# Moving a layer's modulation loads ahead of its linear attention and loading ready-made bias tables, in a two-layer diffusion trunk

## The chip, the cores and the metric

The kernel runs on one core of one Trainium2 chip. The metric is the device time of one execution in microseconds. Before the change three runs took 1935.68, 1934.28 and 1926.67 us, a median of 1934.28 us.

## The reference

Two layers are applied to 512 latent tokens and 256 context tokens of width 1024, in float32. Each layer mixes tokens by four groups of heads, writes them out by one projection, and ends in a feed-forward block with a convolution in its gate. Cut to what matters here:

```python
for l in range(DEPTH):                       # DEPTH = 2
    ctx_out = l < DEPTH - 1
    mod_l = silu(c) @ w_mod[l] + b_mod[l]    # six vectors of 1024: shift, scale, gate of mixing and of ffn
    mod_c = silu(c_ctx) @ w_mod[l] + b_mod[l]
    hl = rmsnorm(xl, g_pre_mix[l]) * (1 + sc_ml) + sh_ml
    hc = rmsnorm(xc, g_pre_mix[l]) * (1 + sc_mc) + sh_mc
    y_c, y_l = token_mixing(hc @ w_in[l], hl @ w_in[l], ...)     # S5, NA, GLA, SWA side by side
    xl = xl + gt_ml * rmsnorm(y_l @ w_out[l], g_post_mix[l])
    hl = rmsnorm(xl, g_pre_ffn[l]) * (1 + sc_fl) + sh_fl
    xl = xl + gt_fl * rmsnorm(conv_ffn(hl, ...), g_post_ffn[l])
    ...

def na_mixer(...):       # neighbourhood attention: an 8 x 64 grid, blocks of 16 columns, 32 key columns each
    bias = rpb[:, dr, dc]                    # by the difference of rows and of columns
    s_nb = einsum("brnqhd,brnkwhd->bhrnqkw", ql, k_blk) * scale + bias
    s_nb = where(in_win, s_nb, -1e30)        # 16 columns around the query
    s_cx = einsum("brnqhd,bchd->bhrnqc", ql, kc) * scale
    p_nb, p_cx = joint_softmax(s_nb, s_cx)
```

The first third of the modulation (shift and scale ahead of mixing) is wanted at once; the other two thirds, rounds 1 and 2 in the kernel, hold the gate of mixing and what the feed-forward block needs, and are wanted only after `w_out`.

## The kernel before

`mixing` runs a layer's token mixing in stages, one behind the other: the linear attention (GLA, with `gla_core`), the state-space model (S5, eight units made by `s5_unit`), neighbourhood attention (NA, `na_units`, two pairs of heads, four column blocks and the context for each), and windowed attention (SWA). In layer 0 GLA lies at about 164 to 264 us, S5 at 264 to 330 and NA at 330 to 427. The products of the input projection that later stages need are no stage of their own: `project` (L789) queues them as generators in `self.fill`, and `gap(n)` draws n of their steps between the pieces of the attention code, so that PE has work while VectorE (DVE) and ScalarE (ACT) run a softmax or a scan. `need(name)` draws a projection to its end. A second list, `self.later`, holds the modulation: each `gap` ends with `pump(self.rate)`, which takes `rate` steps from it. The rates are r00 in GLA, r01 in S5 and r02 in NA for layer 0 (2, 1 and 2).

`mod_round` (L206) makes one round of modulation: 32 steps, each with one 256 KB load into `wm` (L215, on SP's queue, three buffers) and four matmuls (L218) into one PSUM bank; `mod_end` copies the sum (`modrow`, L226) and transposes it (`modt`, L229). Rounds 1 and 2 of layer 0 become available at `mods()` (L1405 and L1445 in `mixing`), which before stands at the beginning of S5, so that their 64 steps are drawn in S5 and NA; a `pump(1000)` at the beginning of SWA draws what is left. PSUM has eight banks in three groups: two for the dense sums (tag "d"), four for the attentions' inner products (tag "m"), and two for their outputs (tag "o"). The modulation's sum takes one with tag "o".

`run_units` (L539) runs a list of units in a pipeline: it starts a unit, calls `gap`, and then carries the unit before to its next piece. In S5 a unit's first half makes `bu` (L853), its second half `s5o` (L884), copies that to `s5zz` (L885, two buffers of its own) and stores it. `s5_end` loads the stored result, loads `w_glu` (L901, ACT's queue), and applies the gate.

`na_table` (L974) makes the bias of one head: eight loads of 24 KB from a padded copy of `na_rpb` (`nawide`, L981, ACT's queue), each with a window that slides by partition, and three adds on GpSimd (POOL, L985) of a window mask that is loaded once a layer (`namask`, L1477). `na_units` makes two tables for each pair of heads, copies the queries from row order into block order (`nqb`, L1057, ACT), and then yields four units (`na_unit`: scores `nas` L1028, table add and maximum L1034, exponential L1036, transposition `napt` L1043, output `nao` L1049). The rotary tables of SWA's `rope` are loaded on ACT's queue (L1075).

The order of instructions on each engine is not written out by hand: a scheduler sets it, by a simulated timeline, from the order of the program, the waits and the buffers. Names in the rows: `pd` is a dense sum, `gA` and `go` GLA's scores and outputs, `gS` its state, `gms` its norm, `lap` and `la` its gates, `tp` a transposition, `gp` SWA's gate rows, `co` and `cs` the context attention, `glu` S5's gate, `pka` S5's operands, built by the kernel and kept in `s5ops` in device memory.

Of the kernel before, what the change touches and what calls it, by code (L numbers as in the profile page):

```python
# [10 lines left out]
FT = mybir.dt.float32  # L11
# [25 lines left out]
KN = dict(build=(1, 1, 1, 2, 1, 1, 1, 1, 2, 1, 1), build1=0, r00=2, r01=1, r02=2, r10=0, r11=3, r12=1, glaA=1, glaB=1, s5=2, s5b=2, na1=0, na2=1, sw1=1, sw2=2, swA=4, pump=6, rows=2, d4=2, ahead=3000, s5n=3, gt=2, six=1, bg=1, wat=(0, 2, 4, 6), wmb=5, go0=12, s5e=4, resA=1, resB=0, slow=1, slow0=5, ro1=2, ro2=2)  # L37
# [4 lines left out]
C_SP, C_SN, C_NA, C_COS, C_SIN, C_ALL = 384, 512, 640, 1408, 1920, 2432  # L42
# [17 lines left out]
def constants():  # L60
    c = np.zeros((128, C_ALL), np.float32)
    i = np.arange(128)
    c[:, C_ID:C_ID + 128] = np.eye(128)
    same = (i[:, None] // 64) == (i[None, :] // 64)
    c[:, C_BD:C_BD + 128] = same / 64.0
    c[:, C_G:C_G + 64] = i[:, None] % 64 <= i[None, :64]
    c[:, C_G + 64:C_G + 128] = i[:, None] % 64 >= i[None, :64]
    c[:, C_SP:C_SP + 128] = np.where(i[None, :] >= i[:, None], 0.0, NEG)
    c[:, C_SN:C_SN + 128] = np.where(i[None, :] <= i[:, None], 0.0, NEG)
    for t, b in enumerate((0, 1, 3)):  # L70
        col = 16 * b + i % 16
        ws = np.clip(col - 8, 0, 48)
        kc = NA_OFF[b] + np.arange(256) % 32
        ok = (kc[None, :] >= ws[:, None]) & (kc[None, :] < ws[:, None] + 16)
        c[:, C_NA + 256 * t:C_NA + 256 * (t + 1)] = np.where(ok, 0.0, NEG)
    t = np.arange(512)
    inv = (np.float32(10000.0) ** (-np.arange(0, 32, 2, dtype=np.float32) / np.float32(32))).astype(np.float32)
    d = i % 64
    pos = np.where((d < 32)[:, None], (t // 64)[None, :], (t % 64)[None, :]).astype(np.float32)
    ang = (pos * inv[d % 16][:, None]).astype(np.float32).astype(np.float64)  # L80
    c[:, C_COS:C_COS + 512] = np.cos(ang)
    c[:, C_SIN:C_SIN + 512] = np.sin(ang) * np.where((d % 32) < 16, -1.0, 1.0)[:, None]
    return c


class Trunk:
# [118 lines left out]
    def mod_round(self, l, r, pool, tag="o"):  # L205
# [6 lines left out]
        for i in range(4 * KT):  # L212
            k, c = i // 4, i % 4
            w = pool.tile([128, 512], FT, name="wm", tag="wm", bufs=3)
            nc.sync.dma_start(w, self.a["w_mod"][l, 128 * k:128 * (k + 1), 2048 * r + 512 * c:2048 * r + 512 * c + 512])  # L215
# [323 lines left out]
    def run_units(self, units, gaps):  # L539

        last = None
        for u in list(units) + [None]:
            if u is not None:
                next(u)
            for n in gaps:
# [243 lines left out]
    def project(self, l, H, name, cols, chunks, scale=1.0, o=None):  # L789

        def steps():
            w = self.w_in(l, cols)
            t = self.R[name] = o or self.p3(name)
            for c0, cn in chunks:
                p = self.ps("pd", "d")[:, :cn]
                yield from self.dense_steps(w, H, c0, cn, p)
                self.nc.scalar.mul(t[:, c0:c0 + cn], p, scale)
# [43 lines left out]
    def s5_unit(self, l, r, U, ops, zd, ctx_out):  # L841
# [43 lines left out]
        z = mp.tile([128, 2, 96], FT, name="s5zz", tag="s5zz", bufs=2)  # L885
# [6 lines left out]
    def s5_end(self, l, zd, Y, ctx_out):  # L892
# [8 lines left out]
        nc.scalar.dma_start(wg, a["s5_w_glu"][l].rearrange("(k p) m -> p k m", p=128))  # L901
# [168 lines left out]
    def rope(self):  # L1070
# [3 lines left out]
        for c, o in zip(cs, (C_COS, C_SIN)):  # L1074
            nc.scalar.dma_start(c, self.a["cpack"][:, o:o + 512])  # L1075
# [262 lines left out]
    def mixing(self, l, H, ctx_out):  # L1338
# [66 lines left out]
        mods = lambda: self.later.extend([self.chain([self.mod_round(0, r, self.wm) for r in (1, 2)])] if l == 0 else [])  # L1405
# [46 lines left out]
        mods()  # L1452
# [12 lines left out]
        self.run_units(units, (KN['s5b'] if l else KN['s5'],))  # L1465
# [10 lines left out]
        mk = self.mp.tile([128, NT], FT, name="namask")  # L1476
        nc.scalar.dma_start(mk, a["cpack"][:, C_NA:C_NA + 768])  # L1477
# [375 lines left out]
```

## Time and profile before

| | us |
|---|---|
| median of three runs | 1934.28 |
| the profiled execution | 1929.45 |
| its span in the profile | 1927.7 |
| TensorE (PE) busy, 11705 matmuls | 1790.8 |
| its weight loads (PEld, beside PE) | 1465.3 |
| VectorE (DVE) | 1167.0 |
| ScalarE (ACT) | 727.1 |
| GpSimd (POOL) | 157.3 |

The span is one execution on one core, taken by the hardware profiler. A busy time is the sum of an engine's instructions and says nothing of what waits for what: engines work beside each other. A long busy PE can still be PE at half its speed, so the granted clock is read beside it: 1.00 is 2.4 GHz, 0.50 is 1.2 GHz, and a stretch between has both. The mean over the execution is 0.954. Idle time of an engine counts only where the chain of waits runs through it. Instructions that issue a transfer occupy the issuing engine's queue for a while (SP, ACT and POOL issue here) and the transfer lands later.

### The profile page before, as it was taken

The page shows a single profiled execution, that of the slowest core. Times are in us where ns is not written, and L with a number is a line of the kernel's source. Part 1 is how long each engine was busy: PE and PEld are TensorE (multiplying, and loading weights), DVE is VectorE, ACT ScalarE, POOL GpSimd, SP SyncE. Part 2 cuts the span into 40 slices and gives each one's busy share as a digit, 9 for nine tenths or more (in the row PEclk, how much of TensorE's full clock was granted, in tenths as well). Part 3 has the DMA queues.
Part 4 walks back from the last instruction along what each step waited for, and adds up shares of the span by engine and source line. Part 5 has one row for each costly group of instructions (what it writes and reads, how often), then busy time and mean ns, then how long its engine had stood idle before and what let it go on. Part 6 is the DMA issues. An engine that isn't in the chain of part 4 may idle for free.

```text
span 1927.7 us, 30566 instructions
## 1 busy us (share of the span) xinstructions
PE 1790.8 (93%) x11705; PEld 1465.3 (76%) x11705; DVE 1167.0 (61%) x2793; ACT 727.1 (38%) x1486; POOL 157.3 (8%) x236
## 2 busy tenths in 40 slices
PE   4899989798998999999999997999798989999997
PEld 2888768565678888888888877877576688888885
DVE  5796655653779946864843474766464654444446
ACT  5334412543664323222222254642354643323222
POOL 5121000100111000000000020000100100000001
PEclk7999889898998999999999998999898999999999
DMA  9264146444123434543533132326322043323232
GB/s 305 65 173 128 40 132 188 113 138 133 64 88 116 151 103 137 170 134 112 165 117 99 56 119 91 95 82 174 79 70 78 23 133 112 106 83 114 77 117 79
DMA packets 243185, 219.79 MB, mean 114 GB/s; under 512 B 45324, under 2 KB 187590, under 8 KB 243040
## 3 DMA queue, kind: packets, MB, share of 16 engines
q1 hardware_dynamic: 225600, 198.52, 34.0%
q0 software_dynamic: 6528, 15.06, 2.7%
q10 hardware_dynamic: 10912, 4.26, 1.4%
q8 instruction: 92, 1.51, 0.3%
q14 instruction: 53, 0.43, 0.1%
HBM read 190.27 MB, written 27.53 MB: 113 GB/s over the span
## 4 chain that ended last, share of the span: by engine, by line
PE 78%; DVE 8%; DMA 7%; ACT 3%; issue 2%; SPq 1%; POOL 1%; ACTq 0%; DVEq 0%; POOLq 0%
PE pd L471 28%; PE pd L312 20%; PE pd L482 12%; DMA wm<-in_w_mod_dram 3%; PE pd L509 2%; PE nao L1049 1%; DVE wlo L275 1%; PE swo L1164 1%; PE go L1279 1%; DMA nawide<-in_rpb_pad_dram 1%; DMA pka<-s5ops 1%; PE s5o L884 1%; PE go L1282 1%; PE swpt L1152 1%; PE napt L1043 1%
## 5 line engine op out<-in xcount | busy, mean ns | idle before, releaser
L275 DVE TENSOR_TENSOR wlo<-wst,whi 128x1024 fp32r<-128x1024 f32 x190 | 232.9, 1226 | 247.5 <-ACT whi L274 236.6
L274 ACT CAST whi<-wst 128x1024 fp32r<-128x1024 f32 x190 | 199.5, 1050 | 423.6 <-PE pd L471 124.9
L312 PE MATMUL pd<-whi,hidh 128*128 128x512 f32 x440 | 171.8, 392 | 1.7 <-DVE za L352 1.6
L312 PE MATMUL pd<-whi,hidl 128*128 128x512 f32 x440 | 171.5, 390 | 0.0
L312 PE MATMUL pd<-wlo,hidh 128*128 128x512 f32 x440 | 170.6, 390 | 0.0
L312 PEld LDWEIGHTS pd<-whi,hidh 128*128 128x128 f32 x440 | 82.6, 188 | 20.6 <-DVE za L352 2.9
L312 PEld LDWEIGHTS pd<-wlo,hidh 128*128 128x128 f32 x440 | 82.6, 188 | 17.5
L312 PEld LDWEIGHTS pd<-whi,hidl 128*128 128x128 f32 x440 | 82.6, 188 | 17.1
L196 DVE SCALAR_TENSOR_TENSOR macc<-wm,cT,macc 128x512 f32<-128x512 f32 x112 | 82.3, 748 | 19.6 <-DMA wm<-in_w_mod_dram 18.9
L1578 DVE TENSOR_TENSOR fg<-fg,pd 128x512 f32<-128x512 f32 x64 | 38.5, 602 | 64.8 <-PE pd L471 63.6
L1577 ACT ACTIVATE fg<-fg 128x512 f32<-128x512 f32 x66 | 36.8, 559 | 105.7 <-DVE fg L1576 101.9
L1628 DVE TENSOR_TENSOR za<-za,pd 128x512 f32<-128x512 f32 (+1 forms) x40 | 21.9, 552 | 72.1 <-PE pd L312 72.1
L1574 ACT ACTIVATE fg<-pd,vb 128x512 f32<-128x512 f32 x64 | 39.4, 618 | 46.0 <-PE pd L471 46.0
L363 POOL TENSOR_TENSOR za<-za,g 128x768 f32<-128x768 f32 x10 | 18.8, 1882 | 413.1 <-ACT sq L353 382.9
L1575 DVE SCALAR_TENSOR_TENSOR fg<-pd,vb,fg 128x511 f32<-128x511 f32 x64 | 42.2, 661 | 15.6 <-ACT fg L1574 15.6
L274 ACT CAST hidh<-fg 128x512 fp32r<-128x512 f32 x66 | 36.1, 547 | 36.5 <-DVE fg L1578 36.1
L471 PE MATMUL pd<-h0h,whi 128*128 128x512 f32 (+1 forms) x118 | 43.7, 370 | 4.7 <-DVE fg L1576 2.9
L471 PE MATMUL pd<-h0h,wlo 128*128 128x512 f32 (+1 forms) x118 | 42.4, 359 | 4.5 <-DVE wlo L275 4.5
L275 DVE TENSOR_TENSOR hidl<-fg,hidh 128x512 fp32r<-128x512 f32 x66 | 39.2, 597 | 7.0 <-ACT hidh L274 6.9
L1576 DVE SCALAR_TENSOR_TENSOR fg<-pd,vb,fg 128x511 f32<-128x511 f32 x64 | 42.5, 663 | 1.2
L218 PE MATMUL modp<-wm,cT 128*32 128x128 f32 x512 | 28.9, 313 | 14.9 <-DMA wm<-in_w_mod_dram 12.8
L471 PE MATMUL pd<-h1h,whi 128*128 128x512 f32 (+1 forms) x118 | 42.4, 360 | 0.0
(694 smaller groups left out, 5212.4 us busy)
## 6 DMA issues: line engine op xcount, KB each, us to landing
wst<-in_ffn_w_up_dram SPq DMA_DIRECT2D x88, 512.0 KB
wm<-in_w_mod_dram SPq DMA_DIRECT2D x160, 256.0 KB
wst<-in_ffn_w_down_dram SPq DMA_DIRECT2D x44, 512.0 KB
wst<-in_w_in_dram SPq DMA_DIRECT2D x36, 512.0 KB
pka<-s5ops SPq DMA_DIRECT2D x16, 544.0 KB
wm<-in_w_mod_dram SPq DMA_DIRECT2D x16, 512.0 KB
wst<-in_w_out_dram SPq DMA_DIRECT2D x12, 512.0 KB
xres<-za SPq DMA_DIRECT2D x16, 384.0 KB
```

The costliest lines, as they stand in the source:

```text
L196: nc.vector.scalar_tensor_tensor(o, w, self.cT[:, k, s:s + 1], o, op0=OP.mult, op1=OP.add)
L274: nc.scalar.copy(hi, src)
L275: return nc.vector.tensor_tensor(lo, src, hi.bitcast(FT), op=OP.subtract)
L312: self.nc.tensor.matmul(o, ht[:, sl], wp[:, i, :], start=j == 0 and x == 0, stop=j == n - 1 and x == 2)
L471: nc.tensor.matmul(o, wt[:, j, ms], ht[:, c0:c0 + cn], start=j == 0 and i == 0, stop=j == len(ks) - 1 and i == 2)
L482: nc.tensor.matmul(o, wt[:, j, ms], ht[:, c0:c0 + cn], start=j == 0 and i == 0, stop=j == len(ks) - 1 and i == 2)
L509: self.nc.tensor.matmul(o, wt[:, k, :], ht[:, sl], start=(first and k == 0 and x == 0), stop=(k == KT - 1 and x == 2), skip_group_check=True)
L1574: nc.scalar.mul(g, p, cw(1))
L1575: nc.vector.scalar_tensor_tensor(g[:, 1:cn], p[:, 0:cn - 1], cw(0), g[:, 1:cn], op0=OP.mult, op1=OP.add)
L1576: nc.vector.scalar_tensor_tensor(g[:, 0:cn - 1], p[:, 1:cn], cw(2), g[:, 0:cn - 1], op0=OP.mult, op1=OP.add)
L1577: nc.scalar.activation(g, g, AF.Gelu_apprx_tanh)
L1578: nc.vector.tensor_tensor(g, g, p2, op=OP.mult)
```

## The change

Six things change. Rounds 1 and 2 of layer 0's modulation become available before GLA's first gap instead of at S5, three steps to a gap (r00 = 3), loaded on POOL's queue, and their sum takes a bank with tag "m". The bias tables of NA are made ahead on the host, masked and laid out by head, and loaded whole, 384 KB a head, by POOL's queue; the loads of `nawide` and `namask`, POOL's adds and the mask constants are gone. The projection of NA's queries writes block order itself, so `nqb` is gone. Behind S5's first unit `run_units` makes a further gap of three steps in layer 0 and one in layer 1, and the `rope` filler is held back until S5 is over. `s5zz` takes a buffer of the `wm` pool. `w_glu` and the rotary tables are loaded on POOL's queue.

```diff
-KN = dict(..., r00=2, r01=1, r02=2, ...)
+KN = dict(..., r00=3, r01=1, r02=2, ...)
...
 def mod_round(self, l, r, pool, tag="o"):
             w = pool.tile([128, 512], FT, name="wm", tag="wm", bufs=3)
-            nc.sync.dma_start(w, self.a["w_mod"][l, 128 * k:128 * (k + 1), 2048 * r + 512 * c:2048 * r + 512 * c + 512])
+            nc.gpsimd.dma_start(w, self.a["w_mod"][l, 128 * k:128 * (k + 1), 2048 * r + 512 * c:2048 * r + 512 * c + 512])
...
-    def run_units(self, units, gaps):
+    def run_units(self, units, gaps, first=0):
         last = None
         for u in list(units) + [None]:
             if u is not None:
                 next(u)
+            if first:
+                self.gap(first)
+                first = 0
             for n in gaps:
                 self.gap(n)
...
     def project(...):
-                self.nc.scalar.mul(t[:, c0:c0 + cn], p, scale)
+                if blocks and c0 == 0:
+                    self.nc.scalar.mul(t[:, 0:SEQ].rearrange("p (b r c) -> p b r c", b=4, r=8),
+                                       p.rearrange("p (r b c) -> p b r c", r=8, b=4), scale)
+                else:
+                    self.nc.scalar.mul(t[:, c0:c0 + cn], p, scale)
...
 def s5_unit(...):
-        z = mp.tile([128, 2, 96], FT, name="s5zz", tag="s5zz", bufs=2)
+        z = self.wm.tile([128, 512], FT, name="s5zz", tag="wm", bufs=3)[:, 0:192].rearrange("p (g n) -> p g n", g=2)
...
 def s5_end(...):
-        nc.scalar.dma_start(wg, a["s5_w_glu"][l].rearrange("(k p) m -> p k m", p=128))
+        nc.gpsimd.dma_start(wg, a["s5_w_glu"][l].rearrange("(k p) m -> p k m", p=128))
...
-    def na_table(self, l, h, mk):
-        tb = mp.tile([128, 3, 256], FT, name="natab", tag="natab", bufs=3)
-        w = mp.tile([128, 8, 48], FT, name="nawide", tag="nawide", bufs=1)
-        for r in range(8):
-            nc.scalar.dma_start(w[16 * r:16 * r + 16], bass.AP(...))
-        for t, o in enumerate((16, 8, 0)):
-            nc.gpsimd.tensor_tensor(tb[:, t]..., w[:, :, 47 - o:...:-1], mk[:, 256 * t:256 * t + 256]..., op=OP.add)
-        return tb
+    def na_tables(self, l):
+        T = []
+        for h in range(4):
+            tb = self.mp.tile([128, 3, 256], FT, name="natab", tag="natab", bufs=4)
+            self.nc.gpsimd.dma_start(tb, self.a["na_tab"][l, h])
+            T.append(tb)
+        return T
...
-        self.project(l, H, f"nq{hp}", [(W_NQ + c, 128)], own, 0.125)
+        self.project(l, H, f"nq{hp}", [(W_NQ + c, 128)], own, 0.125, blocks=True)
...
-        qb = self.p3("nqb")[:, 0:SEQ]
-        self.nc.scalar.copy(qb.rearrange("p (b r c) -> p b r c", b=4, r=8), by(q[:, 0:SEQ]))
...
 def rope(...):
-            nc.scalar.dma_start(c, self.a["cpack"][:, o:o + 512])
+            nc.gpsimd.dma_start(c, self.a["cpack"][:, o:o + 512])
...
 def mixing(...):
-        mods = lambda: self.later.extend([self.chain([self.mod_round(0, r, self.wm) for r in (1, 2)])] if l == 0 else [])
+        mods = lambda: self.later.extend([self.chain([self.mod_round(0, r, self.wm, "m") for r in (1, 2)])] if l == 0 else [])
+        mods()
         self.rate = KN[f"r{l}0"]
...
         self.rate = KN[f"r{l}1"]
-        mods()
         ph = phase("s5")
...
+        hold = [f for f in self.fill if f[0] == "rope"]
+        self.fill = [f for f in self.fill if f[0] != "rope"]
-        self.run_units(units, (KN['s5b'] if l else KN['s5'],))
+        self.run_units(units, (KN['s5b'] if l else KN['s5'],), 1 if l else 3)
+        self.fill += hold
...
-        mk = self.mp.tile([128, NT], FT, name="namask")
-        nc.scalar.dma_start(mk, a["cpack"][:, C_NA:C_NA + 768])
+        tb = self.na_tables(l)
```

The change moves instructions on PE. In layer 0's GLA the products of a chunk before the change, where the hole between `gA` and `go` lies (`gA` and `go` are the scores and outputs, `lap` and `tp` small products of the gates and of the values):

```order
L1264 MATMUL gA<-gqd,gkd 64x64 x4
L1279 MATMUL go<-gAb,gv 64x128
L1264 MATMUL gA<-gqd,gkd 64x64 x4
L1279 MATMUL go<-gAb,gv 64x128
L1204 MATMUL lap<-ggt,wg_840 128x512
L1204 MATMUL lap<-ggt,wg_840 128x256
L1323 MATMUL tp<-consts,gv_1310 128x128 x4
L1282 MATMUL go<-gqd,gS 64x64 x4
L1279 MATMUL go<-gAb,gv 64x128 x2
L1282 MATMUL go<-gqd,gS 64x64 x4
```

In the changed kernel such a place in layer 0's GLA reads so:

```order
L1256 MATMUL gA<-gqd,gkd 64x64 x8
L212 MATMUL modp<-wm,cT 32x128 x4
L1271 MATMUL go<-gAb,gv 64x128
L1256 MATMUL gA<-gqd,gkd 64x64 x3
L212 MATMUL modp<-wm,cT 32x128 x4
L1256 MATMUL gA<-gqd,gkd 64x64 x5
L212 MATMUL modp<-wm,cT 32x128 x4
L1271 MATMUL go<-gAb,gv 64x128
L1274 MATMUL go<-gqd,gS 64x64 x4
L1271 MATMUL go<-gAb,gv 64x128 x2
```

Steps of the modulation (`modp`, four matmuls each) now stand among the scores and outputs; 53 of the 64 stand in GLA. At the beginning of S5, PE had before the change:

```order
L1293 MATMUL gms<-gsq,consts 128x256
L853 MATMUL bu<-s5u_2659,pka 64x96 x8
L218 MATMUL modp<-wm,cT 32x128 x24
L853 MATMUL bu<-s5u_2659,pka 64x96 x8
L884 MATMUL s5o<-s5u_2659,pkb 128x96
L884 MATMUL s5o<-s5h_2934,pkb 128x96 x2
```

and has in the changed kernel:

```order
L1285 MATMUL gms<-gsq,consts 128x256
L854 MATMUL bu<-s5u_2924,pka 64x96 x8
L212 MATMUL modp<-wm,cT 32x128 x16
L854 MATMUL bu<-s5u_2924,pka 64x96 x8
L885 MATMUL s5o<-s5u_2924,pkb 128x96
L885 MATMUL s5o<-s5h_3271,pkb 128x96 x2
```

Four modulation steps instead of six stand behind the first `bu`, and no dense products have come in there. Between NA and SWA of layer 0, PE had before:

```order
L1323 MATMUL tp<-consts,sv 128x128 x5
L935 MATMUL cs<-sk,sq_3406 128x256 x4
L218 MATMUL modp<-wm,cT 32x128 x48
L229 MATMUL modt<-consts,modrow 128x128 x4
L970 MATMUL co<-ptb,navw 64x256 x4
```

and has in the changed kernel:

```order
L1315 MATMUL tp<-consts,sv 128x128 x6
L965 MATMUL cpt<-consts,pe 128x128 x2
L971 MATMUL co<-ptb,navw 64x256
L936 MATMUL cs<-sk,sq_3702 128x256
```

The twelve modulation steps and the transposition of their sum are gone from there.

## Rows read from the trace of the kernel before

**Rows 1.** The page: busy times by engine, and the chain that ended last.

```profile
PE 1790.8 (93%) x11705; PEld 1465.3 (76%) x11705; DVE 1167.0 (61%) x2793; ACT 727.1 (38%) x1486; POOL 157.3 (8%) x236
...
PE 78%; DVE 8%; DMA 7%; ACT 3%; issue 2%; SPq 1%; POOL 1%; ACTq 0%; DVEq 0%; POOLq 0%
```

**Rows 2.** Windows: stretch, length, busy us (instructions) by engine, PE clock, DMA share, GB/s.

```profile
164.00:264.00 100.00, 97.66 (x1003) 77.89 (x1001) 61.57 (x116) 38.99 (x71) 4.96 (x13) 0.95 0.20 56
203.00:219.00 16.00, 13.66 (x146) 8.65 (x140) 12.04 (x26) 7.59 (x14) 0.78 (x2) 0.68 0.23 50
264.00:291.00 27.00, 18.28 (x188) 13.62 (x187) 22.49 (x45) 3.07 (x8) 0.40 (x4) 0.68 0.74 238
291.00:330.00 39.00, 38.38 (x310) 33.45 (x309) 24.20 (x50) 6.24 (x14) 0.00 (x0) 1.00 0.61 181
...
342.00:362.00 20.00, 10.20 (x72) 5.81 (x70) 11.99 (x40) 14.24 (x24) 4.48 (x6) 0.67 0.67 133
362.00:427.00 65.00, 64.55 (x558) 42.31 (x556) 40.91 (x134) 31.14 (x74) 2.08 (x3) 0.97 0.38 118
427.00:451.00 24.00, 15.84 (x167) 7.36 (x155) 5.41 (x14) 3.94 (x15) 0.50 (x2) 0.72 0.42 133
1363.00:1387.00 24.00, 11.06 (x53) 7.88 (x53) 5.06 (x17) 7.82 (x15) 3.32 (x5) 0.70 0.42 83
100.00:120.00 20.00, 20.00 (x132) 16.86 (x132) 19.47 (x51) 6.78 (x9) 6.57 (x9) 1.00 0.68 192
```

**Rows 3.** Chain of waits, 325 to 362: start, us, what.

```profile
340.75 3.67 DMA nawide<-in_rpb_pad_dram
...
344.49 2.09 POOL natab L985 x3
...
349.87 3.74 DMA nawide<-in_rpb_pad_dram
...
353.94 2.41 POOL natab L985 x3
```

**Rows 4.** Chain of waits, 362 to 455: first and last of four modulation loads.

```profile
427.51 4.28 DMA wm<-in_w_mod_dram
...
439.71 2.90 DMA wm<-in_w_mod_dram
```

**Rows 5.** Chain of waits, 1360 to 1392, layer 1.

```profile
1367.67 5.88 DMA wst<-in_w_out_dram
...
1373.94 2.14 DMA nawide<-in_rpb_pad_dram
...
1381.36 1.91 DMA nawide<-in_rpb_pad_dram
1383.29 1.28 ACT L1036
```

**Rows 6.** Chain of waits, 195 to 275: the hole in GLA, and S5's start.

```profile
203.75 0.29 DVE gS L1250
...
207.75 0.40 PE go L1279 x2
...
271.20 5.76 DMA pka<-s5ops
```

**Rows 7.** One line's instructions, L981: xcount, ns min/median/max, first to last start.

```profile
L981 ACTq DMA_DIRECT2D nawide<-in_rpb_pad_dram x64: 317/452/1406, 325.9 to 1399.7; - x64
```

**Rows 8.** Windows of L218 alone: PE and PEld busy (records), PE clock, DMA, GB/s.

```profile
264.00:330.00 66.00, 6.44 (x120) 3.32 (x120) 0.87 0.67 204
...
362.00:427.00 65.00, 11.21 (x224) 5.29 (x224) 0.97 0.38 118
427.00:451.00 24.00, 7.80 (x116) 2.44 (x104) 0.72 0.42 133
```

**Rows 9.** One line's instructions, L754: issue in ns, and us to landing.

```profile
L754 POOL DMA_DIRECT2D s5ops<-pin x16: 540/550/555, 117.7 to 964.5; - x16
...
DMA to landing us min/median/max: 2.3/3.4/5.4
```

**Rows 10.** One line's instructions, L1057: the copies of the queries.

```profile
L1057 ACT COPY nqb<-nq x4: 601/626/659, 343.7 to 1377.7; 128x512 f32<-128x512 f32 x4
```

More of the change, by code (lines that the diff above doesn't have):

```diff
@@ L36 @@
 RATES = ((2, 0, 2), (1, 0, 2))
-KN = dict(build=(1, 1, 1, 2, 1, 1, 1, 1, 2, 1, 1), build1=0, r00=2, r01=1, r02=2, r10=0, r11=3, r12=1, glaA=1, glaB=1, s5=2, s5b=2, na1=0, na2=1, sw1=1, sw2=2, swA=4, pump=6, rows=2, d4=2, ahead=3000, s5n=3, gt=2, six=1, bg=1, wat=(0, 2, 4, 6), wmb=5, go0=12, s5e=4, resA=1, resB=0, slow=1, slow0=5, ro1=2, ro2=2)
+KN = dict(build=(1, 1, 1, 2, 1, 1, 1, 1, 2, 1, 1), build1=0, r00=3, r01=1, r02=2, r10=0, r11=3, r12=1, glaA=1, glaB=1, s5=2, s5b=2, na1=0, na2=1, sw1=1, sw2=2, swA=4, pump=6, rows=2, d4=2, ahead=3000, s5n=3, gt=2, six=1, bg=1, wat=(0, 2, 4, 6), wmb=5, go0=12, s5e=4, resA=1, resB=0, slow=1, slow0=5, ro1=2, ro2=2)
 NEG = -1e30
 C_ID, C_BD, C_G, C_RES = 0, 128, 256, 384
-C_SP, C_SN, C_NA, C_COS, C_SIN, C_ALL = 384, 512, 640, 1408, 1920, 2432
+C_SP, C_SN, C_COS, C_SIN, C_ALL = 384, 512, 640, 1152, 1664
 W_A, W_NQ, W_NK, W_NV = 0, 256, 512, 768
@@ L69, in constants @@
     c[:, C_SN:C_SN + 128] = np.where(i[None, :] <= i[:, None], 0.0, NEG)
[L70 to L75, printed above, removed]
     t = np.arange(512)
@@ L787, in w_in, with project @@
         return self.weights(pieces, 8, 128)
-    def project(self, l, H, name, cols, chunks, scale=1.0, o=None):
+    def project(self, l, H, name, cols, chunks, scale=1.0, o=None, blocks=False):
         def steps():
@@ L1049, in na_unit, with na_units @@
                 nc.tensor.matmul(po[sl, 128 * b:128 * b + 128], vv, pb[:, i, 128 * j:128 * j + 128], start=(j == 0), stop=(j == 3))
-    def na_units(self, l, hp, mk, Y, ctx_out):
-        tb = [self.na_table(l, 2 * hp + i, mk) for i in range(2)]
+    def na_units(self, l, hp, tb, Y, ctx_out):
         self.need(f"nv{hp}")
         q, k, v = [self.R[f"n{x}{hp}"] for x in "qkv"]
-        qb = self.p3("nqb")[:, 0:SEQ]
         by = lambda x: x.rearrange("p (r b c) -> p b r c", r=8, b=4)
-        self.nc.scalar.copy(qb.rearrange("p (b r c) -> p b r c", b=4, r=8), by(q[:, 0:SEQ]))
         Vw, Vc = self.na_values(v)
@@ L1060, in na_units @@
         for b in range(4):
-            yield self.na_unit(b, qb, k, Vw, Vc, tb, po)
+            yield self.na_unit(b, q, k, Vw, Vc, tb, po)
         def finish():
@@ L1483, in units @@
             for hp in range(2):
-                for u in self.na_units(l, hp, mk, Y[2 + hp], ctx_out):
+                for u in self.na_units(l, hp, tb[2 * hp:2 * hp + 2], Y[2 + hp], ctx_out):
                     if i == KN["s5e"]:
@@ L1829, in host_arrays @@
     rpb = np.asarray(inputs["na_rpb"])
-    pad = np.zeros((DEPTH, 4 * 465 + 32), rpb.dtype)
-    pad[:, 16:16 + 4 * 465] = rpb[..., ::-1].reshape(DEPTH, 4 * 465)
-    arrays["rpb_pad"] = pad
+    qr, qc, kr, kc = np.ix_(range(8), range(16), range(8), range(32))
+    tab = []
+    for b in (0, 1, 3):
+        q, k = 16 * b + qc, NA_OFF[b] + kc
+        first = np.clip(q - 8, 0, 48)
+        ok = (k >= first) & (k < first + 16)
+        t = np.where(ok, rpb[:, :, kr - qr + 7, np.clip(k - q, -15, 15) + 15], rpb.dtype.type(NEG))
+        tab.append(t.reshape(DEPTH, 4, 128, 256))
+    arrays["na_tab"] = np.ascontiguousarray(np.concatenate(tab, -1))
     arrays["cpack"] = constants()
```

7 lines of the change are left out of this document (removed).

## Prediction

> **What bounds the kernel now.** I read the page's busy times and the chain of waits first: TensorE (PE) is busy for 1790.8 of 1927.7 us and carries 78% of the chain that ended last, transfers 7%, VectorE 8% [rows 1]. So time can be won only where PE stands still or runs below its full clock. That is seen in the table of windows: its columns give PE's busy time and the clock granted to it, and busy time times clock is the work done, in us at full speed. A window's length less that product is its lost time. Six windows of layer 0's mixing and one of layer 1's are read so [rows 2]: 20 − 10.20 × 0.67 = 13.2 us are lost in 342 to 362 (neighbourhood attention, NA, begins); 24 − 15.84 × 0.72 = 12.6 in 427 to 451 (between NA and windowed attention); 24 − 11.06 × 0.70 = 16.3 in 1363 to 1387 (layer 1's NA begins); 16 − 13.66 × 0.68 = 6.7 in 203 to 219 (a hole in the linear attention, GLA); 27 − 18.28 × 0.68 = 14.6 in 264 to 291 (S5 begins). The clock falls (0.67 to 0.72) just where PE had idled before, so a hole costs more than the idle time in it. In 291 to 330 and 362 to 427 PE is busy for 38.38 of 39 and 64.55 of 65 us: there only less work for PE helps.
>
> The chain says what each hole waits for. Layer 0's NA waits in turns for the 24 KB bias loads on ScalarE's (ACT's) queue (3.67, 3.74 us) and for GpSimd's (POOL's) three adds (2.09, 2.41 us) [rows 3]. The stretch before windowed attention waits four times for a 256 KB modulation load, 4.28 us for the first and 2.90 for the last [rows 4]. Layer 1's NA waits for a weight load, then for the bias loads again and for an ACT operation of 1.28 us that stands behind their issues [rows 5]. The GLA hole is VectorE's state chain: from `gS` at 203.75 to the `go` products at 207.75, and what follows runs at the low clock [rows 6]. S5 begins behind the 544 KB `pka` load [rows 6], which the change leaves alone: its 14.6 us stay.
>
> **The change part by part.** *Tables.* 64 loads leave ACT's queue (452 ns of issue each in the median, 1406 at most) [rows 7], and with them 24 adds on POOL and two mask loads; four 384 KB loads on POOL's queue come in. No PE work changes. Of layer 0's 13.2 lost us some remain: the first unit still goes through scores, table add, maximum, exponential and transposition before its output product, PE starts at a low clock, and the first unit's VectorE work now has the six rotary multiplications among it. I take −9, bounds −5 and −13. Layer 1 loses 16.3, but its chain has a weight load of 5.88 us ahead of the first bias load that the change does not touch [rows 5]: −12 less what becomes visible behind it; I take −10, bounds −4 and −14.
>
> *Modulation moves.* 64 steps of one 256 KB load and four products (eight records of PE each). Before, none are in GLA; 120/8 = 15 are in 264 to 330, 224/8 = 28 in 362 to 427, and 116/8 = 14.5 in 427 to 451 [rows 8]. In the new order, 53 stand in GLA and 11 in S5, none behind it. The hole of 427 to 451 loses its cause: −10, bounds −6 (the turn to the next attention still costs something) and −12.6 (all). The steps' own PE time, 6.44/15 = 0.43 us each in S5 and 11.21/28 = 0.40 in NA [rows 8], only moves: 53 × 0.40 = 21 us are added in GLA, and as much goes from S5 (4 steps), NA (28), 427 to 451 (14.5) and the rest from between S5 and NA; the lost times above hold none of it, so 0, bounds −2 and +2 for the difference of 0.03 a step. In GLA the steps fall into lost time in part: 100 − 97.66 × 0.95 = 7.2 us are lost there [rows 2], 6.7 of them by the hole. Three steps per gap give PE work in it, but VectorE's state chain still orders GLA's own products: −3, bounds 0 and −6.7. Their sum sits in one of the four PSUM banks that GLA's scores and sums take in turn, which no row shows with three: +1, bounds 0 and, by the hole as the nearest wait of these products, +6.7.
>
> *Loads on POOL's queue.* PE takes its instructions in order, so a step whose load has not landed stops everything behind it, GLA's products too. There is no row of this load on this queue. The nearest is the 256 KB store to `s5ops`, on the same queue: 550 ns to issue, 2.3/3.4/5.4 us to land [rows 9]. With three buffers, one step each (0.55 + 3.4 + 0.4)/3 = 1.45 us can be had; 53 steps in 117 us (GLA's 100 and most of the 21 that they add) need one per 2.2 us. On average it fits, in a burst of three per gap not always. Lower bound 0; upper bound, every step served alone, (0.55 + 3.4) × 53 = 209 us, of which 117 lie beside GLA: +92. The likely value is near the lower end, since the mean need is below the supply: +4. The S5 stores now share these three buffers: 11 steps are left there, and I count +1, bounds 0 and +11 (1 us each).
>
> *Queries by blocks.* Four ACT copies of 626 ns go [rows 10]; two of them stood ahead of the first products of their pair: −1, bounds 0 and −2.5. *Fillers behind S5's first unit.* The new order shows the same groups of projection products around S5's first units as before: 0. *`wglu` and the rotary tables* change queue: 0 as long as POOL's queue, with four table loads ahead of them, delivers before the gate needs them, in the middle of NA; if it does not, the price is in the second rival.
>
> Sum: −9 − 10 − 10 − 3 + 1 + 4 + 1 − 1 = −27 us. Against the profiled execution (1929.45 us, 1.7 of it around the span) that is 1902. The median of the runs before is 4.8 us higher than it, and they spread over 9 us; I put the forecast at 1904, between the two. A measurement can tell about 0.5%, 9.7 us, from no change: under 1924.6 is faster, over 1944.0 slower.
>
> **Rivals.** *First, the loads starve PE in GLA: slower.* Without the waits (+4 and +1) the sum is −32. Waits in 53 steps eat that up at 32/53 = 0.60 us each, and the result is slower by 0.5% at (32 + 9.7)/53 = 0.79 us. Against it stands that three buffers supply one per 1.45 us; for it, that bursts of three need them within one short gap, that a bad landing of 5.4 us is twice the gap between steps [rows 9], and that POOL's own waits (its memsets for GLA stand between the loads) delay the next issue. At 1.3 us of wait a step: 1934 − 32 + 69 = 1971. Chance 0.13; 1944 to 2000. The trace speaks on one way into this: the 16 issues of the store took 540 to 555 ns at all times [rows 9], the first of them in a window (100 to 120) in which VectorE was busy for 19.47 of 20 us [rows 2]. The Trainium skill, page "SBUF — State Buffer", section "A bandwidth-pool intuition that's wrong (but worth ruling out)", says that such a transfer, about 620 ns alone, takes about 3100 ns beside a VectorE copy, since GpSimd cannot write its descriptors meanwhile; by that figure, as an estimate, 53 loads would take 164 us, longer than GLA, and this rival would be the forecast; the trace does not agree.
>
> *Second, the tables come late.* All four wait behind the last modulation load on POOL's queue, and for S5's tiles to come free; 4 × 384 KB at the 238 GB/s of the busiest window here [rows 2] are 6.6 us, and two tables are needed for the first unit. If layer 0's table wait stays whole and half of layer 1's, 9 + 5 come back: 1904 + 14 = 1918, chance 0.15, 1908 to 1926.
>
> *Third, NA lacks cover.* The 28 steps in 362 to 427 were work for PE while a unit's softmax ran on VectorE and ACT (40.91 and 31.14 of 65 us busy) [rows 2]. If units then wait on each other, the 11.21 us come back as idle time, and some at a low clock: 1904 + 11 = 1915, up to 1926. Chance 0.2.
>
> *Fourth, the fillers behind S5's first unit do what they are there for.* The order shows none of them; if the chip's timing made them count, at most the rest of S5's 14.6 us of lost time would go: 1904 − 14.6 = 1889. Chance 0.03.
>
> **How the numbers follow.** The forecast has 0.47, the third rival 0.2, the second 0.15, the first 0.13, the fourth 0.03, and 0.02 stay for nothing told. The forecast's own range goes by the bounds: all holes closed is −13 − 14 − 12.6 − 2 − 6.7 + 0 − 2.5 = −51, 1883 against the median, and the weak ends (−5 − 4 − 6 + 2 + 6.7, with the waits as taken) make −1; both ends at once are unlikely, and I take 1886 to 1920. The range of 1886 to 1926 leaves out the first rival and the outer edges of the others. Faster by over 0.5%: 0.46 of the forecast, 0.18 of the third, 0.11 of the second and 0.03 of the fourth: 0.78. Slower: the first, 0.13. Same: the rest, 0.09.
>
> **What would show it.** In the changed kernel's windows: GLA longer by some 10 us but PE at 0.95 clock or more in it, with no long PE waits for `wm`; no modulation products behind S5; no idle stretch like 427 to 451, that is at most 3 us between NA's last product and the next dense group; the first NA unit's scores 5 to 9 us sooner after S5's last product, with the `natab` loads landed before. The prediction is wrong if PE's waits for `wm` come to over 35 us, or if NA's window shows PE idle for over 10 us behind VectorE or ACT.

## The result, and the profile after

The changed kernel took 1898.82 us in the median of four runs (1897.74 to 1905.48), beside 1932.12 for the kernel before on the same chip: a ratio of 0.9837, 95% interval 0.9803 to 0.9872. The forecast was 1904. The profiled execution took 1899.37 us, its span is 1897.6. The page's busy times of the changed kernel, against [rows 1]:

```profile
PE 1781.1 (94%) x11705; PEld 1456.5 (77%) x11705; DVE 1163.5 (61%) x2793; ACT 716.9 (38%) x1476; POOL 181.7 (10%) x290
```

PE's work is the same in count, so nearly all of the gain is lost time. To find its place both traces are cut at the same events: GLA's first score, S5's first product, its last product, NA's first output, NA's last, SWA's first output. The windows of the kernel before, layer 0 in five and then layer 1's S5 and its turn to NA (columns as in [rows 2]):

```profile
183.90:266.10 82.20, 78.92 (x862) 60.66 (x857) 46.80 (x102) 27.31 (x50) 4.96 (x13) 0.94 0.15 37
266.10:320.40 54.30, 45.90 (x417) 38.40 (x416) 44.18 (x90) 6.90 (x16) 0.40 (x4) 0.84 0.68 212
320.40:361.50 41.10, 30.88 (x233) 23.52 (x231) 15.33 (x49) 18.96 (x34) 6.80 (x9) 0.84 0.70 162
361.50:429.10 67.60, 67.12 (x581) 43.87 (x583) 41.82 (x134) 31.64 (x75) 2.08 (x3) 0.97 0.39 118
429.10:488.60 59.50, 50.91 (x324) 34.23 (x320) 24.65 (x61) 21.58 (x66) 1.08 (x4) 0.86 0.40 127
1312.10:1363.80 51.70, 49.16 (x383) 42.81 (x382) 41.51 (x81) 12.72 (x22) 0.00 (x0) 0.97 0.64 184
1363.80:1398.30 34.50, 21.56 (x92) 15.95 (x90) 11.31 (x38) 11.47 (x23) 6.75 (x9) 0.75 0.36 64
```

The same seven of the changed kernel:

```profile
184.40:285.30 100.90, 98.22 (x1228) 70.48 (x1224) 50.55 (x107) 27.82 (x50) 29.98 (x60) 1.00 0.54 164
285.30:343.30 58.00, 47.38 (x400) 39.45 (x400) 42.67 (x88) 6.93 (x16) 4.81 (x13) 0.82 0.56 176
343.30:384.00 40.70, 33.14 (x170) 25.32 (x169) 23.81 (x70) 19.52 (x37) 3.97 (x7) 0.84 0.38 122
384.00:438.40 54.40, 53.20 (x326) 35.95 (x326) 30.50 (x110) 28.26 (x68) 0.00 (x0) 0.93 0.00 1
438.40:480.70 42.30, 42.30 (x230) 31.24 (x227) 24.45 (x59) 21.45 (x66) 1.08 (x4) 1.00 0.35 110
1303.70:1350.80 47.10, 47.10 (x382) 40.99 (x381) 40.32 (x80) 10.50 (x19) 0.00 (x0) 1.00 0.70 202
1350.80:1370.90 20.10, 19.02 (x101) 14.13 (x99) 13.35 (x43) 12.66 (x26) 3.05 (x5) 1.00 0.51 163
```

Layer 0 as far as SWA's first output goes from 304.7 us to 296.3, only −8.4: GLA takes 18.7 more, S5 3.7 more, NA 13.2 less, and the stretch behind NA 17.2 less, at full clock and without a gap. The turn from S5 to NA, where I had put −9, is as long as before. Layer 1 gives most of the rest of the 30.1: −4.6 in S5, for which my sum has no term, and −14.4 at the turn, where PE is now busy for 19.02 of 20.10 us at a clock of 1.00. PE's waits say why. In the kernel before, from 1312 to 1399 (engine line waited for: us in total, times, longest):

```profile
PE nvp L1014 <- ACT navw L1009: 6.0, 1, 6.0
PE pd L482 <- ACT sk L797: 3.0, 1, 3.0
PE nvp L1008 <- DVE nvw L1002: 2.9, 1, 2.9
```

In the changed kernel, from 1303 to 1371, the largest is

```profile
PE nvp L1003 <- DVE nvw L997: 0.7, 2, 0.5
```

So PE had not waited there for the tables: two of these three waits, 9.0 us, were for ACT's ordinary copies (`navw`, `sk`), which stood behind the small loads' issues on ACT. ACT's timeline of the kernel before shows it:

```profile
1368.54 5.84 ACTq L981 DMA_DIRECT2D nawide<-in_rpb_pad_dram  x7
1374.70 0.58 ACT L1009 COPY navw<-nvp 128x512 f32<-128x512 f32 x1 [9.17 <-DMA nawide<-in_rpb_pad_dram]
...
1378.61 4.65 ACTq L981 DMA_DIRECT2D nawide<-in_rpb_pad_dram  x8
...
1385.31 0.85 ACT L797 ACTIVATE sk<-pd 128x512 f32<-128x512 f32 x2
```

The third, 2.9 us, was for VectorE's copies `nvw`, which waited for S5's last store to land:

```profile
1367.06 0.90 DVE L1002 COPY nvw<-nv 128x256 f32<-128x256 f32 x4 [0.27 <-DMA s5zd<-s5zz]
```

Layer 0's turn still has waits, in 343 to 385:

```profile
PE napt L1038 <- DVE nass L1033: 3.0, 1, 3.0
PE nas L1023 <- DVE mod L227: 2.1, 1, 2.1
PE nvp L1009 <- ACT navw L1004: 1.7, 1, 1.7
```

and VectorE's timeline there shows the first unit's table adds, and nothing but other work before its maximum and the negation that the exponential needs:

```profile
371.83 0.42 DVE L1027 CUSTOM_DVE_ANT_0 nass<-nas,natab 128x256 f32<-128x256 f32 x1
...
372.78 1.28 DVE L1072 TENSOR_TENSOR sq<-sq,rope 128x512 f32<-128x512 f32 x2
...
374.15 1.28 DVE L1071 TENSOR_TENSOR rp<-rp,rope 128x512 f32<-128x512 f32 x2
375.35 0.47 DVE L1029 TENSOR_SCALAR_CACHE_REDUCE nass<-nas,m 128x256 f32<-128x256 f32 x1
...
378.14 0.14 DVE L1030 TENSOR_SCALAR m<-m 128x1 f32<-128x1 f32 x1
```

Rotary work (`rp`, `sk`, `sq`), 4.8 us of it, makes up most of what lies between, and the exponential begins 6 us after the table adds. The first rival did not come: the 64 loads on POOL's queue were issued in 536 to 577 ns each and landed in 3.4 us in the median, and PE waited for them in GLA four times, 2.2 us in all, and in S5 three times, 3.9 us (3.8 us before):

```profile
L209 POOL DMA_DIRECT2D wm<-in_w_mod_dram x64: 536/536/577, 82.4 to 333.0; - x64
...
DMA to landing us min/median/max: 2.9/3.4/6.2
```

(The call of `mods()` at S5's beginning is at L1452 of the listing of before, not at L1445.)

### The profile page after: what moved, and what is told of

Its sections match the earlier page's. It is cut to its first block, busy times and chain, and to the rows that moved or that the text cites. A ratio compares the mean times of both kernels' runs of the same rounds, so it can differ in the third digit from the quotient of the medians.

```text
span 1897.6 us, 30442 instructions
## 1 busy us (share of the span) xinstructions
PE 1781.1 (94%) x11705; PEld 1456.5 (77%) x11705; DVE 1163.5 (61%) x2793; ACT 716.9 (38%) x1476; POOL 181.7 (10%) x290
## 4 chain that ended last, share of the span: by engine, by line
PE 60%; DVE 6%; ACT 2%; DMA 2%; issue 1%; POOL 0%; DVEq 0%; SPq 0%; ACTq 0%; POOLq 0%
PE pd L465 29%; PE pd L306 17%; PE pd L476 6%; PE pd L503 1%; DVE wlo L269 1%; DVE za L384 1%; PE swo L1156 1%; PE xt L409 1%; PE s5o L885 1%; ACT sq L389 1%; DVE ru L252 0%; PE nao L1044 0%; PE napt L1038 0%; PE go L1271 0%; DMA xo<-xres 0%
## 5 line engine op out<-in xcount | busy, mean ns | idle before, releaser
L306 PEld LDWEIGHTS pd<-wlo,hidh 128*128 128x128 f32 x440 | 82.6, 188 | 17.6
L190 DVE SCALAR_TENSOR_TENSOR macc<-wm,cT,macc 128x512 f32<-128x512 f32 x112 | 81.7, 745 | 18.0 <-DMA wm<-in_w_mod_dram 17.6
L357 POOL TENSOR_TENSOR za<-za,g 128x768 f32<-128x768 f32 x10 | 18.8, 1883 | 415.7 <-ACT sq L347 385.4
L209 POOL DMA_DIRECT2D wm<-in_w_mod_dram x64 | 34.3, 538 | 126.0 <-PE modp L212 82.8
L1570 DVE SCALAR_TENSOR_TENSOR fg<-pd,vb,fg 128x511 f32<-128x511 f32 x64 | 42.4, 663 | 1.2
L465 PE MATMUL pd<-h1h,whi 128*128 128x512 f32 (+1 forms) x118 | 42.4, 359 | 0.0
```

The lines of the kernel that those rows point to most:

```text
L190: nc.vector.scalar_tensor_tensor(o, w, self.cT[:, k, s:s + 1], o, op0=OP.mult, op1=OP.add)
L209: nc.gpsimd.dma_start(w, self.a["w_mod"][l, 128 * k:128 * (k + 1), 2048 * r + 512 * c:2048 * r + 512 * c + 512])
L306: self.nc.tensor.matmul(o, ht[:, sl], wp[:, i, :], start=j == 0 and x == 0, stop=j == n - 1 and x == 2)
L465: nc.tensor.matmul(o, wt[:, j, ms], ht[:, c0:c0 + cn], start=j == 0 and i == 0, stop=j == len(ks) - 1 and i == 2)
L1570: nc.vector.scalar_tensor_tensor(g[:, 0:cn - 1], p[:, 1:cn], cw(2), g[:, 0:cn - 1], op0=OP.mult, op1=OP.add)
```

## The experiments

Twelve kernels, each timed in three rounds beside the kernel before, in three sets. Its median was 1928.64, 1928.02 and 1928.46 us there, so ratios are compared: 0.001 is 1.9 us. The ranges in the expectations were set from the times of earlier sets, so that a time a few us from a bound decides nothing by itself. One profile was taken of each kernel. Times of layers are read at the events above, layer 1 from GLA's first score to SWA's last output (295.3 us before, 272.5 changed).

**The tables, and the modulation, each alone and each undone.** First:

```diff
 (kernel before)
-        tb = [self.na_table(l, 2 * hp + i, mk) for i in range(2)]
+        tb = self.na_tables(l)   # once a layer, host-made na_tab
```

> The kernel before with the ready-made tables on POOL's queue and nothing else. Theory (the tables' cost before was ACT standing behind the small loads, so that PE waited for ACT's other copies): layer 1 loses nothing at the turn from S5 to NA any more, 18.8 us gained between S5's last product and NA's first output, and layer 0 gains up to 9 there; 1903 to 1913 us in all. Rival (layer 1's gain comes from the held rotary work and the further gap behind S5's first unit): layer 1 gains at most 8, and the time is 1918 to 1926 us.

Measured 1915.80 us, 0.9932 (0.9907 to 0.9956): a time between the two ranges. Layer 1 falls by 17.6 us to 277.7, more than the rival's 8; 11.6 of this lie at the turn, where the theory had 18.8. PE's waits for `navw` and `sk` on ACT are gone there, as the theory had it, and the wait for VectorE's copies is left:

```profile
PE nvp L1002 <- DVE nvw L996: 2.9, 1, 2.9
```

Layer 0 gains nothing: 368.7 us from GLA's first score to SWA's last output, 368.1 before. Its NA is 5.8 us shorter, with 176 records of modulation for 232 (8 to a step), and the stretch behind, where the last steps are drained, 6.0 longer, with 120 for 96. The turn takes 41.0 us for 41.1. By length less busy time times clock, 11.1 us are lost in it for 15.2 before, but 6.1 for 2.5 in NA:

```profile
321.00:362.00 41.00, 32.45 (x271) 24.92 (x271) 20.14 (x60) 17.89 (x36) 2.18 (x4) 0.92 0.64 199
362.00:423.80 61.80, 59.27 (x502) 38.95 (x502) 35.10 (x122) 29.63 (x71) 0.00 (x0) 0.94 0.30 96
```

```diff
 (changed kernel)
-        tb = self.na_tables(l)
+        tb = [self.na_table(l, 2 * hp + i, mk) for i in range(2)]   # 64 loads on ACT, 24 adds on POOL
```

> The changed kernel with the tables made as before (64 small loads on ACT's queue, adds on POOL, mask loads), all else as changed. Theory (tables carry the larger part): 18 to 26 us come back, 1917 to 1925 us, most of it in layer 1. Rival (the other parts carry layer 1): 5 to 10 us come back, 1904 to 1909 us.

Measured 1920.67 us, 0.9957 (0.9936 to 0.9978), 23 us by ratio: the theory. Layer 1 takes 286.2 us, 13.7 more, and layer 0 is 9.0 us longer, 3.3 of it at the turn. PE's wait for ACT's copy in layer 1 is back:

```profile
PE nvp L1021 <- ACT navw L1016: 4.2, 1, 4.2
```

```diff
 (kernel before)
-            nc.sync.dma_start(w, self.a["w_mod"]...)
+            nc.gpsimd.dma_start(w, self.a["w_mod"]...)
...
+        mods()   # ahead of GLA, tag "m", r00=3; not at S5
```

> The kernel before with modulation rounds 1 and 2 begun ahead of GLA, three steps a gap, loads on POOL's queue, the sum in a bank with tag m, and nothing else. Theory: the hole between NA and SWA (15.9 us lost) and GLA's hole (5.5 of 8.2) go, some is given back in NA and S5 where the steps had covered waits: 1914 to 1924 us. Rival (without the steps NA's table wait is barer, so that the move alone gives little): 1924 to 1932 us.

Measured 1920.73 us, 0.9967 (0.9945 to 0.9988). The place of the gain is the theory's: the stretch behind NA is 42.4 us, as in the changed kernel. Its size is not: 1920.73 us lies in the theory's range, but the kernel before took 1928.64 here, and 6 us by ratio are nearer to the rival. S5 is 62.5 us long (54.3 before), with waits of PE of 7.8 us for modulation loads and 5.5 for `pka` loads, and layer 0 as a whole is only 1.7 us shorter in this profile. Layer 1, the same code as before, took 289.0 us here and 295.3 before, so one profile's layer is uncertain by some 6 us.

```diff
 (changed kernel)
-        mods()   # ahead of GLA
...
+        mods()   # at S5; SP's queue, tag "o", r00=2, s5zz in S5's own two buffers
```

> The changed kernel with the modulation as before (begun at S5, two steps a gap in GLA's rate, SP's queue, tag o, the store tiles of S5 in two buffers of their own), all else as changed. Theory: 8 to 18 us come back, 1907 to 1917 us, in the stretch from NA's last output to SWA and in GLA. Rival (layer 0's gain is from the tables, not from this): under 5 us come back, 1899 to 1904 us.

Measured 1928.17 us, 0.9994 (0.9979 to 1.0010): 30 us come back, far more than the theory's 8 to 18, though the modulation alone had gained 6. Of the 30, 18.0 lie in layer 0 of the profile and 11.3 in layer 1, which has none of these modulation steps. This edit also gives S5's store tiles their own buffers back, and keeps the further gap; the next set takes these apart.

**The small parts.**

```diff
 (changed kernel)
-        z = self.wm.tile([128, 512], FT, name="s5zz", tag="wm", bufs=3)[:, 0:192]...
+        z = mp.tile([128, 2, 96], FT, name="s5zz", tag="s5zz", bufs=2)
```

> The changed kernel with S5's store tiles in two buffers of S5's own pool, as before, all else as changed. Theory (NA's first tiles take the place of S5's pool, so VectorE's copies for NA's values wait for the last store of S5 to land; out of that pool they do not): PE's wait for the value copies of about 2.9 us comes back in layer 1 and with it the low clock, 4 to 11 us in all, 1903 to 1910 us. Rival (the store tiles in the modulation's buffers cost waits, as I forecast): the time falls by 0 to 4 us, 1895 to 1899 us, and PE's waits for modulation loads in S5 get shorter.

Measured 1912.40 us, 0.9929 (0.9904 to 0.9955): 18 us slower by ratio than with the shared buffers, the theory's direction and more than its size, though the two intervals leave some 9 to 26. The chain at layer 1's turn shows the mechanism, S5's last store landing before VectorE may write NA's first tiles:

```profile
1354.07 0.27 ACT s5zz L887
...
1354.99 1.94 DMA s5zd<-s5zz
...
1356.96 0.05 DVEq L997
```

and PE's wait is there again (`PE nvp L1003 <- DVE nvw L997` 3.2 us). It stands at layer 1's turn in all five kernels here whose store tiles have their own buffers (2.9 to 3.2 us) and is at most 0.7 us in the nine where they share. Layer 1's S5 also goes with it: 48.8 to 52.4 us in the five, 47.1 to 48.6 in the nine. In the trace the layer-1 turn costs 2.8 us and layer 0's S5 4.7, where PE waits 8.1 us for modulation loads instead of 3.9, against the rival; layer 0's turn is 3.6 us shorter. The rest of the 18 is not located, and this profile's own time, 1906.7, is the lowest of its runs.

```diff
 (changed kernel)
-        self.run_units(units, (KN['s5b'] if l else KN['s5'],), 1 if l else 3)
+        self.run_units(units, (KN['s5b'] if l else KN['s5'],))
```

> The changed kernel without the further gap behind S5's first unit, all else as changed. Theory (as forecast, the gap does nothing that counts): 1896 to 1902 us, layer 1's S5 still at 47 to 48 us. Rival (the gap is why layer 1's S5 has no wait for its operands): S5 of layer 1 gets 2 to 5 us longer with waits of PE for the operand loads, 1901 to 1906 us.

Measured 1889.80 us, 0.9811 (0.9785 to 0.9836), below both ranges. By ratio that is 5 us less than the changed kernel, and the two intervals overlap; but the profile shows where the gap costs time, in layer 0, and layer 1's S5 stays at 47.1 us without it. Windows of this kernel, S5 to NA's end:

```profile
287.10:341.10 54.00, 45.60 (x393) 38.43 (x392) 42.64 (x88) 7.02 (x16) 4.28 (x12) 0.87 0.59 185
341.10:371.40 30.30, 28.11 (x176) 22.58 (x174) 18.27 (x55) 18.96 (x33) 4.51 (x8) 1.00 0.48 155
371.40:428.50 57.10, 51.83 (x329) 35.27 (x328) 35.68 (x126) 31.76 (x74) 0.00 (x0) 0.97 0.04 10
```

S5 is 4.0 us shorter than in the changed kernel, the turn 10.4 shorter, NA 2.7 longer. With the gap all 96 dense products left (`pd`) stand ahead of NA's first scores; without it 69 do, and 27 stand behind them, beside the first softmax. In the kernel before, and with the tables alone, all 96 stand ahead too, and the turn is as long there as with the gap (41.1 and 41.0 us); which of the other changes lets 27 of them move behind was not tried.

```diff
 (changed kernel)
-        hold = [f for f in self.fill if f[0] == "rope"]
-        self.fill = [f for f in self.fill if f[0] != "rope"]
...
-        self.fill += hold
```

> The changed kernel with the rotary filler drawn in its old place, all else as changed. Theory (its six multiplications stand among the first unit's VectorE work because the scheduler finds them ready there, not because they are held): same order there, 1896 to 1902 us. Rival (holding puts them there): layer 0's first NA output comes 3 to 6 us sooner after S5, 1893 to 1896 us.

Measured 1896.74 us, 0.9847 (0.9808 to 0.9885). The order is the theory's: the rotary work still stands between the first unit's table adds (379.0) and its negation (384.4). The first output came 2.4 us sooner after S5 and GLA took 7 longer, so that time and profile show no gain either way.

```diff
 (changed kernel)
-            nc.gpsimd.dma_start(w, self.a["w_mod"]...)
+            nc.sync.dma_start(w, self.a["w_mod"]...)
```

> The changed kernel with the modulation loads on SP's queue, all else as changed. Theory (POOL's queue costs 0.54 us of issue and the waits in S5, SP's has to share with S5's operand loads): in GLA no difference, in S5 up to 4 us longer, since S5's operand loads queue behind waiting modulation loads; 1898 to 1906 us. Rival (the queue does not matter, only when the loads start): 1897 to 1901 us with S5 as in the changed kernel.

Measured 1902.19 us, 0.9876 (0.9853 to 0.9899). S5 is 58.2 us long (58.0 changed). The interval overlaps the changed kernel's; that the queue matters is not shown.

**What the further gap costs, and three combinations.**

```diff
 (changed kernel, run_units)
             for n in gaps:
+                if head and (u is None or u is units[-1]):
+                    n = 0 if u is None else 1
                 self.gap(n)
```

> The changed kernel with layer 0's further gap of three steps kept behind S5's first unit, and three steps fewer drawn behind S5's last units, so that 28 of the dense products stand behind NA's first scores again, as without the further gap, instead of none; layer 1 without its further gap. Theory (the further gap costs since it takes from NA's first softmax the dense products that covered it): as fast as the kernel without the gap, 1886 to 1895 us, with 13 to 14 us from NA's first scores to its first output and no loss of over 3 us there. Rival (the gap costs in S5 itself, where the further steps stand): 1896 to 1901 us, with S5 of layer 0 at 57 us or more.

Measured 1901.14 us, 0.9856 (0.9811 to 0.9901). Windows, S5 to NA's end:

```profile
286.90:345.80 58.90, 48.05 (x401) 40.14 (x400) 42.37 (x88) 7.02 (x16) 4.78 (x13) 0.83 0.57 174
345.80:376.50 30.70, 27.08 (x164) 21.53 (x162) 17.35 (x54) 18.97 (x33) 3.98 (x7) 1.00 0.47 145
376.50:438.80 62.30, 56.84 (x333) 37.66 (x332) 36.83 (x127) 31.68 (x74) 0.00 (x0) 0.89 0.04 9
```

Both are right in part. The 28 products behind the first scores bring the turn to 30.7 us, as without the gap: that they are the turn's cover is shown. S5 stays at 58.9, as the rival had it, so the gap also costs some 4 to 5 us in S5, from a cause not tried. And NA takes 62.3 us, at a clock of 0.89, so that what the turn gained was lost again behind it.

```diff
 (e1_tables_alone)
-        z = mp.tile([128, 2, 96], FT, name="s5zz", tag="s5zz", bufs=2)
+        z = self.wm.tile([128, 512], FT, name="s5zz", tag="wm", bufs=3)[:, 0:192]...
```

> The kernel before with the ready-made tables and with S5's store tiles in the modulation's buffers, and nothing else. Theory (these two parts make all of layer 1's gain): layer 1 from GLA's first product to SWA's last output takes 270 to 275 us, as in the changed kernel (272.5), against 277.7 with the tables alone, without a wait of PE for NA's value copies; 1903 to 1912 us in all. Rival (the store tiles' part comes from layer 0, where the modulation loads are then held back by the stores): layer 1 at 277 to 279 us, layer 0's S5 at 50 us or less.

Layer 1 took 275.0 us and PE's longest wait for NA's value copies was 0.5: the theory, there. But the time is 1917.19 us, 0.9946 (0.9930 to 0.9962), no better than the tables alone, and layer 0 is 8.7 us longer: in S5, where the modulation's loads now share their buffers with the stores, 64 of its records stand for 96, and NA takes 71.3 us for 61.8, with 240 for 176. It seems that the shared buffers pay only with most of the modulation out of S5, but no run changes that alone.

```diff
 (changed kernel without the further gaps)
-KN = dict(..., r00=3, ...)
+KN = dict(..., r00=4, ...)
```

> The changed kernel without the further gaps and with four modulation steps a gap in GLA, so that all 64 stand in GLA and none in S5. Theory (S5's operand loads and the modulation loads stand in each other's way in S5): S5 of layer 0 at 46 to 51 us against 53.9, GLA 4 to 7 us longer, 1882 to 1890 us in all. Rival (three loads at a time are all that GLA can be supplied with): PE waits for modulation loads in GLA come to 5 to 20 us, 1890 to 1905 us.

Measured 1911.76 us, 0.9914 (0.9885 to 0.9943), worse than both, by the rival's mechanism. S5 is 51.6 us, near the theory's, but GLA takes 122.8 at a clock of 0.93, with PE's waits for the loads four times as long as in the changed kernel:

```profile
184.60:307.40 122.80, 110.67 (x1324) 76.53 (x1320) 51.26 (x113) 27.90 (x50) 34.04 (x67) 0.93 0.51 154
```

```profile
PE modp L212 <- DMA wm<-in_w_mod_dram: 9.1, 7, 2.8
```

Three steps a gap were supplied in GLA almost without waits, four were not; whether the three buffers, the loads' landing or POOL's issues set the limit was not tried.

```diff
 (changed kernel without the further gaps, rope)
-            nc.vector.tensor_tensor(x, x, cs[1], op=OP.mult)
+            nc.gpsimd.tensor_tensor(x, x, cs[1], op=OP.mult)   # and the two operations behind it
```

> The changed kernel without the further gaps and with the rotary multiplications and additions on GpSimd instead of VectorE. Theory (they stand among the first units' VectorE work and delay NA's normalising, which PE waits for, 4.4 us): layer 0's NA 2 to 5 us shorter, layer 1 the same, 1884 to 1889 us. Rival (GpSimd and VectorE hold each other up, or SWA waits for the slower engine): 1889 to 1896 us.

Measured 1891.65 us, 0.9805 (0.9771 to 0.9838): NA in layer 0 is 55.5 us for 57.1, less than the theory's gain, in layer 1 55.6 for 58.5, but the time is not told apart from the kernel without the gaps. These two are the fastest: all four runs of each lie below the lowest of the changed kernel (1886.44 to 1893.32 and 1884.98 to 1895.25, against 1897.74), though the kernel before was 4 us faster beside them and the ratios' intervals overlap the changed kernel's.

## Why the prediction was right, and where it was not

The sum, −27, came near the measured −33 by medians and −30 between the profiles, but by luck in part: several of its parts were wrong, in ways that cancelled. By ratio the runs give −13 for the tables alone, −6 for the modulation alone, −18 for the store tiles where the rest is changed, and +5 for the further gap, each with some 4 to 8 us to either side. That these make −32 proves none of them, since they do not simply add: undone in the changed kernel the tables are worth 23 us, and the modulation together with the store tiles 30, while tables and store tiles together gained no more than the tables alone.

- **Layer 0's tables, −9: failed.** Alone they gained nothing there: 4 us less were lost at the turn and 4 us more in NA, as the third rival has it. I took the chain's table waits for the cause of the hole, but the first unit's softmax ends as late without them: rotary work stands in it, and no dense product covers it, in the kernel before as with the further gap. The sign that I named, scores 5 to 9 us sooner, did not come: they begin some 24 us after S5's last product in both. Undone in the changed kernel the tables cost 3.3 us at this turn, so that their worth in layer 0 hangs on the other parts.
- **Layer 1's tables, −10, bounds −4 and −14: rather too small.** Alone −11 to −18, by which profile of the old code one takes, and undone −14. The 5.88 us weight load on the chain, for which I took some off, was no wait of PE; its copies on ACT were.
- **The hole behind NA, −10: too small.** The stretch is 17.2 us shorter, of which the twelve steps moved away are about a third (an estimate, by the 7.80 us of 14.5 steps in [rows 8]); the slow clock had reached past the window that I read, to SWA's first output (0.86 over 59.50 us).
- **GLA's hole, −3:** 82.2 − 78.92 × 0.94 = 8.0 us lost before, 2.7 after. The window lost more in other kernels with the same steps (e7: 107.9 us long), so this part is unsteady.
- **Loads on POOL's queue, +4:** 2.2 us of waits in GLA. The waits of the first rival are near: four steps a gap bring 9.1 us of them, though not its slower kernel.
- **PSUM bank, +1:** not in GLA; PE waited 2.1 us in NA for the bank of the transposed sum.
- **Store tiles, +1: wrong sign.** I counted who shares the three buffers and not who takes the place that they left: about 18 us by ratio with the rest changed, of which the traces place only a part, and nothing with the tables alone.
- **Further gap, 0: it cost time.** I compared the order of products only around S5's first units. Three steps drawn earlier moved 27 products across NA's first scores, far below: some 5 us by ratio (9 by medians), and in the profiles also 4 us of S5, from a cause not tried.
- **Queries by blocks, −1:** PE's waits for `nqb` (1.1 and 0.7 us) are gone; not tried alone.

The second rival did not come: the tables were issued from 344.2 to 345.8 and landed in 7.5 us at most, long before the first add at 371.5. The third came in one place, the first softmax, and not over NA as a whole, where PE is busy for 53.20 of 54.40 us.

## What to carry to other kernels

Ask of a small load not only when it lands but what stands behind its issue on the engine that issues it: here PE's wait was named after ACT's copies. A tile that is moved to another pool also changes what the next stage's first tiles wait for, and a filler drawn earlier is missing later, so an order has to be compared as far as the next place where PE waits. A sum that comes out is no proof of its parts: each part wants a run that undoes it alone.

## What the runs showed of the hardware

Two holes of like length were followed by different clocks. Without the further gap PE waited 4.38 us in NA, ran at a granted clock of 0.57 for the next 4 us and then at 1.00 for 8; with the gap shifted it waited 3.73 us and ran at 0.55 for 12 us and 0.77 for 6 more. The windows of the first, and of the second:

```profile
379.00:383.00 4.00, 4.00 (x20) 2.98 (x20) 1.74 (x6) 2.75 (x7) 0.00 (x0) 0.57 0.00 0
383.00:391.00 8.00, 8.00 (x56) 5.48 (x56) 4.14 (x16) 3.67 (x9) 0.00 (x0) 1.00 0.00 0
```

```profile
384.00:396.00 12.00, 11.49 (x56) 7.65 (x56) 3.72 (x18) 3.98 (x9) 0.00 (x0) 0.55 0.00 0
396.00:402.00 6.00, 6.00 (x21) 3.36 (x20) 2.38 (x6) 3.40 (x8) 0.00 (x0) 0.77 0.00 0
```

The second had one more wait of 0.48 us within its slow stretch; why it lasted three times as long stays open. The 64 loads on POOL's queue took 536 to 577 ns to issue and 2.9/3.4/6.2 us to land, beside a VectorE that was busy for half of GLA (50.55 of 100.90 us); the 16 stores of [rows 9] took 2.3/3.4/5.4 us to land. The Trainium skill, page "SBUF — State Buffer", section "A bandwidth-pool intuition that's wrong (but worth ruling out)", gives 3100 ns instead of 620 for a transfer beside a VectorE `tensor_copy`. No run here shows that case: beside these issues VectorE ran operations of a tensor with a tensor or a scalar, scans and predicated copies, and its only plain copy there (`modrow`) reads PSUM. So when the prediction says that the trace does not agree, it compares issue times beside other work, and the page's figure stays untested.
